# Overlapping window extraction: the index arithmetic ahead of the loads, one copy moved between engines, and the last store as plain transfers

## The chip, the cores and the metric

The kernel runs on one core of one Trainium2 chip. The metric is device time in microseconds (us). The core has the vector engine (DVE), the scalar engine (ACT), GpSimd (POOL) and the sync engine (SP), which work side by side, and sixteen DMA engines that move data between the chip's main memory and the on-chip buffer of 128 partitions. DMAs are issued here by two of them: POOL, whose descriptors are made in software (queue `software_dynamic`), and SP (queue `hardware_dynamic`).

## The reference

The input is an image batch `x[16, 64, 64, 64]` (batch, channel, height, width; float32). Windows of 8 x 8 are cut from it at a stride of 4, so 15 x 15 windows an image, and each is copied out whole, with all channels:

```
for i in range(n_h):
    for j in range(n_w):
        h_start = i * stride
        w_start = j * stride
        result[:, i, j] = x[:, :, h_start:h_start + window_size, w_start:w_start + window_size].copy()
```

No arithmetic is done. 16.8 MB are read and 16 x 225 windows of 16 KB, 59 MB, are written.

## The kernel before

**The image on the chip.** `L` holds all of `x`. A partition holds one channel half `ch` (32 channels), one image `b` and one quarter of the height `q` (16 rows): partition = `ch * 64 + b * 4 + q`. The loads are sorted by batch half `y` (8 images each) and by quarter `q`: for each of the eight pairs, SP loads channels 4 to 31 of the first channel half, and POOL the other four of them and all of the second half. One load thus fills eight partitions, four apart (line 57).

**The tiles that go out.** Four buffers `G[0..3]` of 128 partitions each hold one complete window a partition (64 channels x 8 x 8, 16 KB). Partition `half * 64 + b * 4 + q` holds the window of row `4 * q + s + half` and column `j`, where `s` is 0 or 2. So a pair `(j, s)` is one tile, and 2 x 15 pairs make the output. With `s = 2` the row would be 15 for `half = 1, q = 3`, which does not exist; those 16 partitions have an index that lies out of bounds, so nothing is written for them.

**`fill` (lines 127 to 139)** makes one half of a tile by two copies out of `L`, one for each channel half; its argument `copies` names who makes them (`act` is ACT, `dve` is DVE). For the fourth row of a quarter (`s + half = 3`) the window reaches into the next partition, so a copy of the upper four image rows and a `stream_shuffle` on DVE of the lower four stand in place of one copy.

**`scatter` (lines 114 to 125)** stores a tile by one indirect DMA on POOL's queue, with an index tile that gives each partition its row of the output. The index tiles (`idx` and four variants: `idx_y0`, `idx_y1` for one batch half alone, `idx_hi`, `idx_lo` for the pairs with `s = 2`) come from an `iota` on POOL and some twenty tiny operations on DVE (lines 70 to 107).

**The order.** In the program the loads come first, then iota and index arithmetic, then eight memsets of tile parts that the first stores do not fill, then the tiles. The first three tiles are stored for each batch half separately (six stores of 64 windows: the first three need only the first half's loads, the next three the second's), then 27 whole pairs follow: `j` from 0 to 14, in each `s = 0` (from `j = 3` on) and `s = 2`. Tile number `t` uses buffer `G[t % 4]`, so a fill waits until the store four tiles before has landed. Each engine executes its own instructions in an order that the framework fixes when the kernel is built, which need not be the program's; the framework also sets the waits between engines.

Of the kernel before, what the change touches and what calls it, by code (L numbers as in the profile page):

```python
# [1 line left out]

# [4 lines left out]


@with_exitstack  # L10
def kernel(
    ctx: ExitStack,
    tc: tile.TileContext,
    x: bass.AP,
    window_size: int,
    stride: int,
    out: bass.AP,
):
    nc = tc.nc
    P = nc.NUM_PARTITIONS  # L20

    B, C, H, W = x.shape
    Bo, NH, NW, Co, WSo, WSo2 = out.shape
    WS = int(window_size)
    ST = int(stride)
    assert Bo == B and Co == C and WSo == WS and WSo2 == WS

    f32 = mybir.dt.float32
    i32 = mybir.dt.int32
    ALU = mybir.AluOpType  # L30
    CH = 2
    HQ = P // (B * CH)
    CL = C // CH
    RB = H // HQ
    NSLOT = RB // ST
    NWIN = NH * NW
    CFREE = C * WS * WS
    HP = P // CH
    YB = 8
    NY = B // YB  # L40
    QP = YB * HQ
    assert HQ == 4 and WS == 2 * ST and QP == 32 and NSLOT == 4

    lpool = ctx.enter_context(tc.tile_pool(name="lpool", bufs=1))
    ipool = ctx.enter_context(tc.tile_pool(name="ipool", bufs=1))
    gpool = ctx.enter_context(tc.tile_pool(name="gpool", bufs=1))


    L = lpool.tile([P, CL, RB, W], f32)
    x_v = x.rearrange("(y b) (ch cl) (hq r) w -> ch y hq b cl (r w)", y=NY, ch=CH, hq=HQ)  # L50


    SMALL = 4

    def load(eng, ch, y, q, c0, c1):
        p0 = ch * HP + y * QP + q
        eng.dma_start(out=L[p0 : p0 + QP - HQ + 1 : HQ, c0:c1, :, :], in_=x_v[ch, y, q, :, c0:c1, :])  # L57

    for y in range(NY):
        for q in range(HQ):  # L60
            load(nc.sync, 0, y, q, SMALL, CL)
            load(nc.gpsimd, 0, y, q, 0, SMALL)
            load(nc.gpsimd, 1, y, q, 0, CL)

    def itile(name):
        return ipool.tile([P, 1], i32, name=name)

    pi, tb, tq, tc_, th, idx, idx_y0, idx_y1, idx_lo, idx_hi = (  # L70
        itile(n) for n in ("pi", "tb", "tq", "tc", "th", "idx", "idx_y0", "idx_y1", "idx_lo", "idx_hi")
    )
    FAR = float(2 * B * NWIN)
    nc.gpsimd.iota(pi[:, :], pattern=[[0, 1]], base=0, channel_multiplier=1)  # L74

    def bits(d, shift, mask):
        nc.vector.tensor_scalar(out=d[:, :], in0=pi[:, :], scalar1=shift, scalar2=mask, op0=ALU.logical_shift_right, op1=ALU.bitwise_and)  # L77

    def mul(d, a, m):
        nc.vector.tensor_scalar(out=d[:, :], in0=a[:, :], scalar1=float(m), scalar2=None, op0=ALU.mult)  # L80

    def tt(d, a, b, op):
        nc.vector.tensor_tensor(out=d[:, :], in0=a[:, :], in1=b[:, :], op=op)  # L83

    bits(tb, 2, B - 1)
    bits(tq, 0, HQ - 1)
    bits(tc_, 6, 1)
    mul(tb, tb, NWIN)
    mul(th, tq, NSLOT * NW)
    tt(tb, tb, th, ALU.add)  # L90
    mul(th, tc_, NW)
    tt(idx, tb, th, ALU.add)

    bits(th, 5, 1)
    mul(th, th, FAR)
    tt(idx_y0, idx, th, ALU.add)
    nc.vector.tensor_scalar(out=th[:, :], in0=th[:, :], scalar1=-1.0, scalar2=FAR, op0=ALU.mult, op1=ALU.add)
    tt(idx_y1, idx, th, ALU.add)

    nc.vector.tensor_scalar(out=tq[:, :], in0=tq[:, :], scalar1=float(HQ - 1), scalar2=FAR, op0=ALU.is_equal, op1=ALU.mult)  # L100
    tt(th, tc_, tq, ALU.mult)
    tt(idx_hi, idx, th, ALU.add)
    nc.vector.tensor_scalar(out=tc_[:, :], in0=tc_[:, :], scalar1=-1.0, scalar2=1.0, op0=ALU.mult, op1=ALU.add)  # L103
    tt(th, tc_, tq, ALU.mult)
    tt(idx_lo, tb, th, ALU.add)
    mul(th, tc_, NW)
    tt(idx_lo, idx_lo, th, ALU.add)

    o_v = out.rearrange("b i j c r w -> (b i j) (c r w)")
    nxt = [min(p + 1, 31) for p in range(32)]  # L110
    NG = 4
    G = [gpool.tile([P, C, WS, WS], f32, name=f"G{n}") for n in range(NG)]

    def scatter(g, ix, j, s):
        st = nc.gpsimd.indirect_dma_start(  # L115
            out=o_v,
            out_offset=bass.IndirectOffsetOnAxis(ap=ix[:, 0:1], axis=0),
            in_=g.rearrange("p c r w -> p (c r w)"),
            in_offset=None,
            element_offset=(s * NW + j) * CFREE,  # L120
            bounds_check=B * NWIN - 1,
            oob_is_err=False,
        )
        tc.declare_no_dep(st.ins, group="stores", reason="each store writes rows of its own")
        tc.add_to_no_dep_group("stores", st.ins)

    def fill(g, half, s, j, lo, n, copies):

        d = slice(half * HP + lo, half * HP + lo + n)
        cols = slice(j * ST, j * ST + WS)  # L130
        for ch in (half, 1 - half):
            f = slice(ch * HP + lo, ch * HP + lo + n)
            cs = slice(ch * CL, (ch + 1) * CL)
            copy = copies[ch != half]
            if s < NSLOT - 1:
                copy(out=g[d, cs, :, :], in_=L[f, :, s * ST : s * ST + WS, cols])  # L136
            else:
                copy(out=g[d, cs, 0:ST, :], in_=L[f, :, s * ST : RB, cols])  # L138
                nc.vector.stream_shuffle(out=g[d, cs, ST:WS, :], in_=L[f, :, 0:ST, cols], mask=nxt)  # L139

    act, dve = nc.scalar.copy, nc.vector.tensor_copy

    EARLY = 3
    assert EARLY < NG
    for t in range(NG):
        for half in range(CH):
            p0 = half * HP + (QP if t < EARLY else 0)
            nc.vector.memset(G[t][p0 : p0 + QP, :, :, :], 0.0)  # L150
    t = 0
    for y in range(NY):
        for j in range(EARLY):
            for half in range(CH):
                fill(G[t % NG], half, half, j, y * QP, QP, (act, dve))
            scatter(G[t % NG], (idx_y0, idx_y1)[y], j, 0)
            t += 1

    units = [(j, s) for j in range(NW) for s in (0, 2) if s or j >= EARLY]
    for j, s in units:  # L160
        g = G[t % NG]
        t += 1
        if s == 0:
            for half in range(CH):
                fill(g, half, s + half, j, 0, HP, (act, dve))
            scatter(g, idx, j, s)
        else:

            turn = j % 2
            fill(g, turn, s, j, 0, HP, (act, act))  # L170
            fill(g, 1 - turn, s + 1, j, 0, HP, (dve, dve))
            scatter(g, (idx_hi, idx_lo)[turn], j, s)


# [1 line left out]
_INS = ['x', 'window_size', 'stride']  # L176
_OUTS = [((16, 15, 15, 64, 8, 8), 'float32')]

_NUMBERS = {'window_size': 8, 'stride': 4}


# [26 lines left out]
```

## Time and profile before

| what | value |
|---|---|
| median of 3 runs | 203.56 us (203.37 to 203.70) |
| the profiled execution | 203.62 us, of which the span of the profile is 201.8 |
| DMA, POOL's queue | 68.43 MB, 82.6% of sixteen engines' span |
| DMA, SP's queue | 7.34 MB, 9.4% |
| DVE busy | 131.2 us (65%) in 155 instructions |
| ACT busy | 125.5 us (62%) in 67 |
| POOL busy | 52.6 us (26%) in 54 |
| stores | 33 indirect DMAs on POOL |

The span runs from the first instruction to the last event of the core; the time of a run is a little longer. In rows of instructions in order of time stand the start, the duration, the engine, the line, the operation, its operands and count, and in brackets how long the engine had been idle and what released it. SP's and POOL's work as issuers of DMAs is short beside the transfers themselves, which run on after the issue. The engines' shares are means over the whole run; which engine sets the time has to be read stretch by stretch.

### The profile page before, as it was taken

What the parts mean: (1) busy time and instruction counts of PE and PEld (TensorE: products, weight loads), DVE (VectorE), ACT (ScalarE), POOL (GpSimd) and SP (SyncE); (2) the same over time, 40 slices, a digit from 0 to 9 for tenths busy, and PEclk for the clock granted to TensorE, in tenths of its full rate; (3) what the DMA queues carried; (4) which work ended last, traced back from release to release, by engine and by line L of the source; (5) the groups of instructions that cost most, each with busy time, mean ns of one, the idle gap of its engine ahead of it and who ended that gap; (6) DMA issues with size and microseconds to landing.
All of it is one profiled execution on the core that took longest, in us unless ns stands there. A gap on an engine that the chain in (4) does not pass through costs nothing.

```text
span 201.8 us, 478 instructions
## 1 busy us (share of the span) xinstructions
DVE 131.2 (65%) x155; ACT 125.5 (62%) x67; POOL 52.6 (26%) x54
## 2 busy tenths in 40 slices
DVE  6778888944559999576757765774757577754000
ACT  0000019924259999999977977797777779774000
POOL 7311220200433312613422211323133214311000
DMA  2999999993299899999999999999999999999980
GB/s 93 337 406 399 401 399 400 398 397 98 104 409 406 330 390 412 409 422 416 414 416 429 430 416 416 419 416 432 425 419 416 416 422 432 425 419 414 416 373 36
DMA packets 11476, 75.81 MB, mean 376 GB/s; under 512 B 3776, under 2 KB 3776, under 8 KB 7872
## 3 DMA queue, kind: packets, MB, share of 16 engines
q0 software_dynamic: 9616, 68.43, 82.6%
q1 hardware_dynamic: 1856, 7.34, 9.4%
q14 instruction: 4, 0.03, 0.0%
HBM read 16.78 MB, written 69.21 MB: 426 GB/s over the span
## 4 chain that ended last, share of the span: by engine, by line
DMA 65%; issue 8%; DVE 7%; ACT 7%; POOL 3%; POOLq 1%; DVEq 0%; PEldq 0%; ACTq 0%
DMA out_dram<-G,idx 20%; DMA L<-in_x_dram 16%; DMA out_dram<-G,idx_hi 14%; DMA out_dram<-G,idx_lo 12%; ACT G L136 7%; DVE G L136 4%; DMA out_dram<-G,idx_y 3%; POOL L L57 2%; DVE G L139 2%; POOL out_dram L115 1%; DVE G L138 1%; POOLq L203 1%; DVE th L80 0%; DVE idx_y L83 0%; POOLq L115 0%
## 5 line engine op out<-in xcount | busy, mean ns | idle before, releaser
L136 ACT COPY G<-L 64x2048 f32<-64x2048 f32 (+1 forms) x66 | 124.2, 1896 | 28.9 <-DMA out_dram<-G,idx 10.1
L136 DVE COPY G<-L 64x2048 f32<-64x2048 f32 (+1 forms) x36 | 43.9, 1227 | 22.8 <-DMA out_dram<-G,idx 12.7
L139 DVE STREAM_SHUFFLE G<-L 64x1024 f32<-64x1024 f32 x30 | 38.3, 1276 | 0.0
L138 DVE COPY G<-L 64x1024 f32<-64x1024 f32 x30 | 20.7, 691 | 21.4 <-DMA out_dram<-G,idx_hi 14.4
L150 DVE MEMSET G<- 32x4096 f32 x8 | 27.8, 3472 | 8.0 <-issue 5.4
L115 POOL DMA_INDIRECT out_dram<-G,idx x12 | 13.8, 1149 | 34.7 <-ACT G L136 29.2
L115 POOL DMA_INDIRECT out_dram<-G,idx_hi x8 | 11.7, 1459 | 31.1 <-DVE G L139 17.9
L136 ACT ACT_TABLE_LOAD x1 | 1.3, 1283 | 29.4 <-DMA L<-in_x_dram 29.4
L57 POOL DMA_DIRECT2D L<-in_x_dram x16 | 9.9, 625 | 25.2 <-DMA L<-in_x_dram 24.3
L115 POOL DMA_INDIRECT out_dram<-G,idx_lo x7 | 8.9, 1278 | 18.8 <-ACT G L136 9.7
L115 POOL DMA_INDIRECT out_dram<-G,idx_y x6 | 6.9, 1152 | 22.9 <-DVE tc L103 16.1
L74 POOL IOTA pi<- 128x1 int32 x1 | 1.2, 1230 | 0.1
L83 DVE TENSOR_TENSOR th<-tc,tq 128x1 int32<-128x1 int32 x2 | 0.3, 174 | 0.1
L83 DVE CUSTOM_DVE_ANT_0 idx_y<-idx,th 128x2 uint16<-128x2 uint16 x2 | 0.3, 158 | 0.1
L80 DVE TENSOR_SCALAR th<-tc 128x1 int32<-128x1 int32 x2 | 0.3, 153 | 0.0
L139 DVE LOAD_MASK_SELECT G<-L x30 | 0.2, 6 | 0.0
L83 DVE CUSTOM_DVE_ANT_0 idx_hi<-idx,th 128x2 uint16<-128x2 uint16 x1 | 0.2, 159 | 0.0
L83 DVE CUSTOM_DVE_ANT_0 idx<-tb,th 128x2 uint16<-128x2 uint16 x1 | 0.2, 159 | 0.0
L83 DVE CUSTOM_DVE_ANT_0 idx_lo<-tb,th 128x2 uint16<-128x2 uint16 x1 | 0.2, 159 | 0.0
L83 DVE CUSTOM_DVE_ANT_0 idx_lo<-idx_lo,th 128x2 uint16<-128x2 uint16 x1 | 0.2, 159 | 0.0
L83 DVE CUSTOM_DVE_ANT_0 tb<-tb,th 128x2 uint16<-128x2 uint16 x1 | 0.2, 158 | 0.0
L77 DVE TENSOR_SCALAR th<-pi 128x1 int32<-128x1 int32 x1 | 0.2, 154 | 0.0
(13 smaller groups left out, 1.8 us busy)
## 6 DMA issues: line engine op xcount, KB each, us to landing
L<-in_x_dram POOLq DMA_DIRECT2D x8, 1024.0 KB, 21.2
L<-in_x_dram SPq DMA_DIRECT2D x8, 896.0 KB
L<-in_x_dram POOLq DMA_DIRECT2D x8, 128.0 KB, 21.1
out_dram<-G,idx POOLq DMA_INDIRECT x12, 14.6
out_dram<-G,idx_hi POOLq DMA_INDIRECT x8, 14.0
out_dram<-G,idx_lo POOLq DMA_INDIRECT x7, 14.1
out_dram<-G,idx_y POOLq DMA_INDIRECT x6, 6.3
```

What stands on the lines that cost most here:

```text
L57: eng.dma_start(out=L[p0 : p0 + QP - HQ + 1 : HQ, c0:c1, :, :], in_=x_v[ch, y, q, :, c0:c1, :])
L74: nc.gpsimd.iota(pi[:, :], pattern=[[0, 1]], base=0, channel_multiplier=1)
L77: nc.vector.tensor_scalar(out=d[:, :], in0=pi[:, :], scalar1=shift, scalar2=mask, op0=ALU.logical_shift_right, op1=ALU.bitwise_and)
L80: nc.vector.tensor_scalar(out=d[:, :], in0=a[:, :], scalar1=float(m), scalar2=None, op0=ALU.mult)
L83: nc.vector.tensor_tensor(out=d[:, :], in0=a[:, :], in1=b[:, :], op=op)
L115: st = nc.gpsimd.indirect_dma_start(out=o_v, out_offset=bass.IndirectOffsetOnAxis(ap=ix[:, 0:1], axis=0), in_=g.rearrange("p c r w -> p (c ...
L136: copy(out=g[d, cs, :, :], in_=L[f, :, s * ST : s * ST + WS, cols])
L138: copy(out=g[d, cs, 0:ST, :], in_=L[f, :, s * ST : RB, cols])
L139: nc.vector.stream_shuffle(out=g[d, cs, ST:WS, :], in_=L[f, :, 0:ST, cols], mask=nxt)
L150: nc.vector.memset(G[t][p0 : p0 + QP, :, :, :], 0.0)
L203: with _tile.TileContext(nc) as tc:
```

## The change

Three things change.

1. The block that issues the loads is moved in the program behind the iota and the index arithmetic.
2. In the second batch half, for the second tile (`j == 1`) and its second half, both copies are DVE's; before, one was ACT's and one DVE's.
3. The last two pairs change places, so `(14, 2)` is stored before `(14, 0)`, and this last tile, 128 windows or 2.1 MB, is not stored by the indirect DMA on POOL but by eight plain transfers on SP's queue, one for each quarter and half. Each takes the sixteen partitions of one half that are four apart, one for each image.

```diff
-    for y in range(NY):
-        for q in range(HQ):
-            load(nc.sync, 0, y, q, SMALL, CL)
-            load(nc.gpsimd, 0, y, q, 0, SMALL)
-            load(nc.gpsimd, 1, y, q, 0, CL)
...
     tt(idx_lo, idx_lo, th, ALU.add)

+    for y in range(NY):
+        for q in range(HQ):
+            load(nc.sync, 0, y, q, SMALL, CL)
+            load(nc.gpsimd, 0, y, q, 0, SMALL)
+            load(nc.gpsimd, 1, y, q, 0, CL)
...
+    def free(st):
+        tc.declare_no_dep(st.ins, group="stores", reason="each store writes rows of its own")
+        tc.add_to_no_dep_group("stores", st.ins)
...
             for half in range(CH):
-                fill(G[t % NG], half, half, j, y * QP, QP, (act, dve))
+                copies = (dve, dve) if y and half and j == 1 else (act, dve)
+                fill(G[t % NG], half, half, j, y * QP, QP, copies)
...
     units = [(j, s) for j in range(NW) for s in (0, 2) if s or j >= EARLY]
+    units.append(units.pop(-2))
+    o_q = out.rearrange("b i j c r w -> i j b (c r w)")
...
-            scatter(g, idx, j, s)
+            if (j, s) != units[-1]:
+                scatter(g, idx, j, s)
+                continue
+            g_q = g.rearrange("(ch b q) c r w -> ch q b (c r w)", ch=CH, q=HQ)
+            for q in range(HQ):
+                for half in range(CH):
+                    free(nc.sync.dma_start(out=o_q[q * NSLOT + s + half, j], in_=g_q[half, q]))
```

`free` holds the two lines that `scatter` had: it tells the framework that the stores do not depend on each other.

3 lines of the change are left out of this document (1 added, 2 removed).

## The prediction

> **What bounds the kernel now.** I read four views in this order: the page's forty slices (is one resource full, and where does it fall away), the stretches around the hole that they show, the chain that ended last (who makes the hole), and the instructions in order of time (what each engine did meanwhile).
>
> ```profile
> DMA  2999999993299899999999999999999999999980
> GB/s 93 337 406 399 401 399 400 398 397 98 104 409 406 330 390 412 409 422 416 414 416 429 430 416 416 419 416 432 425 419 416 416 422 432 425 419 414 416 373 36
> ```
>
> The DMA engines are the bound: nine tenths or more in nearly every slice, except the first, slices ten and eleven (98 and 104 GB/s), the small sag at slice fourteen (330) and the last. So time can be won only where the DMA engines stand idle. Columns of the next view: stretch, its length, busy time of DVE, ACT and POOL with counts, granted clock, DMA share, GB/s.
>
> ```profile
> 3.00:4.00 1.00, 1.00 (x1) 0.00 (x0) 1.00 (x2) 1.00 0.49 188
> 4.00:5.00 1.00, 1.00 (x1) 0.00 (x0) 1.00 (x3) 1.00 0.51 197
> ...
> 47.00:48.00 1.00, 0.00 (x0) 0.01 (x1) 0.00 (x0) 1.00 0.08 9
> ...
> 47.30:54.20 6.90, 5.17 (x23) 3.79 (x2) 1.07 (x1) 1.00 0.00 0
> 54.20:54.80 0.60, 0.00 (x0) 0.00 (x0) 0.47 (x1) 1.00 1.03 437
> ...
> 62.40:70.30 7.90, 7.67 (x13) 7.80 (x5) 3.10 (x3) 1.00 0.90 370
> 70.30:71.70 1.40, 1.37 (x4) 1.38 (x2) 0.19 (x1) 1.00 0.66 281
> ...
> 90.00:195.00 105.00, 62.64 (x80) 77.54 (x42) 26.81 (x21) 1.00 1.01 422
> ...
> 195.90:198.10 2.20, 0.00 (x0) 0.00 (x0) 0.00 (x0) 1.00 0.44 186
> ...
> 198.90:201.80 2.90, 0.00 (x0) 0.00 (x0) 0.00 (x0) 1.00 0.00 0
> ```
>
> Loads end at about 47.1 us; then not a byte moves until about 54.6, a hole of 7.5 us. A second, partial loss follows from 62.4 to 71.7: 7.9 x 0.10 + 1.4 x 0.34 = 1.3 us. From 90 to 195 the DMA engines are full at 422 GB/s, while DVE and ACT are busy 63 and 78 of 105 us, so a store of 128 windows (2.10 MB) takes 4.97 us and one of 64 takes 2.49. In that stretch nothing else can set the time: whatever is gained before 72 us is carried to the end unchanged. At the end one half of the engines runs 2.2 us longer than the other (share 0.44), and 2.9 us follow the last byte.
>
> ```profile
> 42.60 5.25 issue
> ...
> 49.29 1.22 DVE G L136
> ...
> 50.54 0.15 DVE tb L77
> ...
> 52.85 0.07 DVE tc L103
> ...
> 52.95 0.40 POOL out_dram L115
> ```
>
> This is the chain, with start and length of each piece: it shows who makes the hole: DVE's last copies of the fourth tile, then the index arithmetic (lines 77 to 103), and only then the first store, since its index tile did not exist. The same stretch in order of time, by engine:
>
> ```profile
> 1.65 3.47 DVE L150 MEMSET G<- 32x4096 f32 x1 [1.65 <-PEq L189]
> 6.04 3.47 DVE L150 MEMSET G<- 32x4096 f32 x1 [0.91 <-issue]
> ...
> 30.69 11.01 ACT L136 COPY G<-L 32x2048 f32<-32x2048 f32 x6
> 34.88 0.66 POOL L57 DMA_DIRECT2D L<-in_x_dram  x1 [4.88 <-DMA L<-in_x_dram]
> 35.63 1.23 POOL L74 IOTA pi<- 128x1 int32 x1
> 35.67 6.93 DVE L136 COPY G<-L 32x2048 f32<-32x2048 f32 x6
> 47.98 3.82 ACT L136 COPY G<-L 32x2048 f32<-32x2048 f32 x2 [6.28 <-issue]
> 48.04 2.47 DVE L136 COPY G<-L 32x2048 f32<-32x2048 f32 x2 [5.44 <-issue]
> ...
> 52.95 1.07 POOL L115 DMA_INDIRECT out_dram<-G,idx_y  x1 [16.09 <-DVE tc L103]
> ...
> 53.56 0.16 DVE L83 CUSTOM_DVE_ANT_0 idx_lo<-idx_lo,th 128x2 uint16<-128x2 uint16 x1
> 57.67 5.12 DVE L136 COPY G<-L 32x2048 f32<-32x2048 f32 x4 [3.96 <-DMA out_dram<-G,idx_y]
> 57.73 17.28 ACT L136 COPY G<-L 32x2048 f32<-32x2048 f32 x9 [5.92 <-DMA out_dram<-G,idx_y]
> ...
> 69.51 0.98 POOL L115 DMA_INDIRECT out_dram<-G,idx_hi  x1 [2.88 <-ACT G L136]
> ```
>
> The three tiles of the first batch half were filled by 42.6, ten microseconds before their first store could go. From 52.95 (issue) to 54.6 (data) a store needs 1.65 us. The first store's landing at 57.67 then releases the tile for the fifth fill.
>
> **Index tiles first.** POOL: the iota, 1.23 us, now stands ahead of the sixteen POOL loads. SP's loads do not wait for it: between 3 and 5 us they alone keep half of the DMA engines busy (0.49, 0.51). So between none and all of 1.23 us is lost to the loads that only POOL carries, the second channel half; I take all of it for copies that read that half, none for the others. DVE: the arithmetic, 50.54 to 53.72 = 3.2 us, moves from behind the eighth copy to the front of the memsets (the first may still precede it, as the iota ends near 2.6). The eight memsets, 4.38 us apart, and the six copies behind them move by 3.2: copies end at 45.8 in place of 42.6. Cover: no store can flow before the loads leave the POOL queue at 47.1. Filled tile by tile, the tiles are ready at 41.2, 43.5 and 45.8, and the third is not needed until 47.1 + 2 x 2.6 - 1.65 = 50.6; if the copies go by halves, the first is ready at 43.5 against 45.4 needed. With that cover gone it would cost up to 3.2. POOL also has to have issued its last load (34.88, now up to 36.1), which is earlier than any of these.
>
> The stores of the first half then run right behind the loads, 47.1 (or up to 48.3) onward, 2.6 each by the spacing of their first landings (57.67, 60.30 below); they land at about 51.4, 54.0 and 56.6 counting the whole 1.23.
>
> ```profile
> 54.33 5.97 DMA out_dram<-G,idx_y
> 60.30 0.02 issue
> ```
>
> The groups of instructions by line and shape give the prices of the copies (after the bar: busy us, then mean ns of one):
>
> ```profile
> L139 DVE STREAM_SHUFFLE G<-L 64x1024 f32<-64x1024 f32 x30 | 38.3, 1276 | 0.0
> ...
> L136 ACT COPY G<-L 32x2048 f32<-32x2048 f32 x12 | 22.4, 1895 | 12.3 <-issue 6.3 <-DMA out_dram<-G,idx_y 5.9
> L138 DVE COPY G<-L 64x1024 f32<-64x1024 f32 x30 | 20.7, 691 | 21.4 <-DMA out_dram<-G,idx_hi 14.4 <-DMA out_dram<-G,idx_lo 6.3
> L136 DVE COPY G<-L 32x2048 f32<-32x2048 f32 x12 | 14.3, 1215 | 9.6 <-issue 5.4 <-DMA out_dram<-G,idx_y 4.0
> ```
>
> What is late next are the fills of the second half. I follow them to the seventh tile (the first of two-row stores, issued at 69.51 now), since from there the queue stays full. **Even copies**: the fifth tile gives one of ACT's two copies to DVE. ACT: three copies of 1.90 from 48.0, to 53.7; the sixth tile's buffer comes free at 54.0, two copies, 57.8; the seventh, two, 61.6. DVE, from 48.04 + 1.23 = 49.3: two, three and two copies of 1.215, to 57.8; the seventh, two of 0.69 + 1.28, to 61.7. Both end together; the store goes at 62.0 (before, ACT's sixth copy from 57.73, at 17.28 / 9 = 1.92 each, ended at 69.25 and POOL started 0.26 later), against 69.51: **7.5 us earlier**. Without the moved copy ACT would take 1.9 longer and end the stage alone at 63.5: the even copies are worth 1.5 to 1.9 of the 7.5.
>
> From the side of the DMA engines: loads to 47.1 (one half of the engines up to 48.3), six stores of 2.5 to 2.6, so 62.5 to 63.9, and the seventh store's data at 62.0 + 1.65 = 63.7. A gap of 0 to 1.2 stands where the 7.5 and 1.3 stood, less the iota's 0 to 1.2: a gain between 6.5 and 8.6, with 7.5 inside. I take 7.5, bounds 6.5 and 8.6.
>
> **The last two units change places; eight plain transfers on SP.** The bytes are the same, no new copy is made, and the fills keep their kinds. SP has nothing queued: the waits of its queue show it idle for 168.4 us at the end of the kernel.
>
> ```profile
> SPq L203 <- DMA out_dram<-G,idx: 168.4, 1, 168.4
> ```
>
> The last store before, from the instructions in order of time:
>
> ```profile
> 184.63 0.97 POOL L115 DMA_INDIRECT out_dram<-G,idx_hi  x1 [4.56 <-ACT G L136]
> ```
>
> The last store is issued at 184.63 now and its last byte leaves 13 us later, so a quicker issue (0.97 us on POOL saved) wins nothing. No row shows 16 KB rows leaving on SP. Dear side: SP's 4 KB pieces moved 188 to 197 GB/s on half of the engines, POOL's stores 211 (half of 422); 2.1 MB at twice 197 take 5.3 in place of 4.97, +0.35. Gainful side: if the eight transfers evened out the two halves' ends, half of 2.2 us: -1.1. Sixteen rows on sixteen engines give each the same share, as the store of 128 did, so I take neither evening nor loss but the half of the dear end: +0.2. A stall that no such row prices is the first rival.
>
> **Sum.** The profiled execution took 203.62 us (span 201.8, 1.8 around it), 0.06 over the median of 203.56, so nothing is corrected: 203.62 - 7.5 + 0.2 = **196.3**.
>
> **Rivals.** (a) *The SP transfers run at half speed.* Each takes sixteen partitions of one half. The rows at 3 to 5 us show eight partitions of one half at 188 to 197 GB/s; they cannot tell whether eight engines or that half's way out of the buffer is the limit. If the latter, 2.1 MB need 10.6 us instead of 4.97. They leave beside POOL's rows, which use the other half's way as well, so between nothing and all of 5.6 is lost: 196.1 to 201.7, in the middle **198.9**. The point is open, since before no two engines had to draw from the same few partitions. Against: halves alternate from one transfer to the next, so some of it can overlap. The Trainium skill states just this ("SBUF — State Buffer", section "Door 1: The DMA port swizzle"): transfers from 64 partitions of one half reach only 8 of 16 ports and half of the rate; by that rule this rival holds, and no run here shows it yet. Chance 0.30.
> (b) *The early stores hold up the loads.* If their rows took turns with the second half's loads in place of queueing behind them, those loads would end up to 7.8 us later (three stores of 2.6), the fills would start at 55 and the seventh store go near 69: about 203. Against it: the loads of the second channel half and the stores are issued by POOL, one behind the other, and only SP's share of the loads could be overtaken. Chance 0.05.
> (c) *The change does not do what it says: the arithmetic stays late on DVE.* In this trace it ran behind eight copies, though the iota was done at 36.9, so an order that was not readiness put it there. Then only the even copies help: ACT's chain shortens by 1.9, and at most the 1.3 of the second loss returns: 202.4. Chance 0.04.
> (d) *Slower: the SP transfers sit on few engines.* A row takes 4.97 / 8 = 0.62 us. On k engines 128 rows take 128/k x 0.62 in place of eight rows. The first 7.3 us of that only eat the gain, so it decides below k = 6.5: on four engines, 32 rows, 14.9 us more, 211. Against: SP's loads of eight partitions filled half of sixteen engines, so partitions do spread. Chance 0.02.
> (e) *Both halves end together*, with the gain at its bound: 195 or less. Chance 0.04.
>
> **Numbers.** The forecast holds with 0.55. Its own range is 195.3 to 197.3. Downward I stop at 195.3 (leaves out e, 0.04); upward the range takes in most of (a), to 200.8, leaving out its worst part (0.05) and (b), (c), (d): 0.20 in all. About 0.4 us (0.2%) is what a measurement of this kernel can tell from no change. Faster: 0.55 + 0.30 + 0.04 + (c) 0.04, and half of (b) 0.02 = 0.95; same: the rest of (b), 0.03; slower: (d), 0.02.
>
> **What would show it.** Index arithmetic on DVE before 10 us, the iota before POOL's first load; the first store issued near 41 to 44; no stretch with DMA share near zero between 45 and 60; the seventh store issued at 62.0, ACT and DVE ending its fill within 0.5 of each other; DMA near 420 GB/s from 72 on. If rival (a) is right, the last 15 us show full DMA share with clearly fewer GB/s. The forecast falls if the fills start later than 49.3, if the DMA hole merely moves to the second half's first store, or if the time from the last SP issue to the end grows.

## The result, and the profile after

The changed kernel runs at 196.82 us (median of 4; before 203.63 beside it), ratio 0.9667 (0.965 to 0.9684), so 6.8 us faster; the forecast was 196.3. The profiled execution took 196.84, its span is 195.1. The page's slices first:

```profile
DMA  2999999999999999999999999999999999999983
GB/s 87 316 403 403 398 402 394 403 399 408 420 375 380 386 420 403 427 420 415 430 430 415 417 417 420 423 423 420 430 423 420 420 427 410 410 418 420 329 259 124
```

The hole of slices ten and eleven is gone. But something new stands at the end: 329 and 259 GB/s at a DMA share that the line above still gives as nine and eight tenths. Instructions of the changed kernel in order of time (start, duration, engine, line):

```profile
0.84 0.12 POOL L68 IOTA pi<- 128x1 int32 x1 [0.39 <-PEq L216]
1.48 5.02 POOL L57 DMA_DIRECT2D L<-in_x_dram  x8 [0.52 <-issue]
...
9.54 0.15 DVE L71 TENSOR_SCALAR tb<-pi 128x1 int32<-128x1 int32 x1
...
38.55 0.16 DVE L77 CUSTOM_DVE_ANT_0 idx_lo<-idx_lo,th 128x2 uint16<-128x2 uint16 x1
38.93 7.00 DVE L139 COPY G<-L 32x2048 f32<-32x2048 f32 x6 [0.22 <-issue]
44.53 1.53 POOL L119 DMA_INDIRECT out_dram<-G,idx_y  x1 [8.54 <-DVE G L139]
...
48.08 28.56 ACT L139 COPY G<-L 32x2048 f32<-32x2048 f32 x15 [5.94 <-issue]
48.13 8.62 DVE L139 COPY G<-L 32x2048 f32<-32x2048 f32 x7 [2.20 <-issue]
...
61.67 0.96 POOL L119 DMA_INDIRECT out_dram<-G,idx_hi  x1 [2.88 <-ACT G L139]
...
171.50 0.96 POOL L119 DMA_INDIRECT out_dram<-G,idx_hi  x1 [3.79 <-ACT G L139]
173.06 3.82 ACT L139 COPY G<-L 64x2048 f32<-64x2048 f32 x2 [2.35 <-DMA out_dram<-G,idx_hi]
...
174.98 14.82 SPq L179 DMA_DIRECT2D out_dram<-G  x8
```

The first store goes at 44.53 (52.95 before), the fills of the second half start at 48.1 as soon as their loads are in, and the seventh store goes at 61.67 (69.51 before): 7.84 us earlier. The stretches of the changed kernel (length, DVE, ACT, POOL, clock, DMA share, GB/s; a row counts whole in the stretch in which it begins, so a share can pass 1):

```profile
47.00:48.00 1.00, 0.00 (x0) 0.00 (x0) 0.69 (x2) 1.00 1.12 447
48.00:54.00 6.00, 5.77 (x5) 5.87 (x4) 3.30 (x2) 1.00 1.03 434
54.00:55.00 1.00, 0.97 (x2) 1.00 (x1) 0.37 (x1) 1.00 0.48 181
...
60.00:65.00 5.00, 4.90 (x8) 4.95 (x3) 0.96 (x1) 1.00 0.89 370
...
72.00:176.00 104.00, 71.21 (x92) 86.76 (x47) 28.69 (x23) 1.00 1.01 421
176.00:179.50 3.50, 0.00 (x0) 0.87 (x1) 0.00 (x0) 1.00 1.03 431
179.50:190.00 10.50, 0.00 (x0) 0.00 (x0) 0.00 (x0) 1.00 0.93 295
190.00:194.00 4.00, 0.00 (x0) 0.00 (x0) 0.00 (x0) 1.00 0.53 164
...
193.90:195.10 1.20, 0.00 (x0) 0.00 (x0) 0.00 (x0) 1.00 0.00 0
```

From 72 to 179.5 full share means 421 to 431 GB/s. Then, with SP's rows among POOL's, a share of 0.93 moves only 295: the engines are occupied but each row takes longer. And behind the last byte 1.2 us follow, where 3.1 did before (last byte at 198.7, span 201.8; the row in the prediction begins a little later, hence its 2.9). So the tail shows a loss and a gain that the total hides.

### The profile page after: what moved, and what is told of

Same layout as the page of the kernel before. It is cut to its first block, busy times and chain, and to the rows that moved or that the text cites. A ratio compares the mean times of both kernels' runs of the same rounds, so it can differ in the third digit from the quotient of the medians.

```text
span 195.1 us, 485 instructions
## 1 busy us (share of the span) xinstructions
DVE 132.0 (68%) x156; ACT 123.6 (63%) x66; POOL 51.8 (27%) x53
## 4 chain that ended last, share of the span: by engine, by line
DMA 66%; DVE 17%; issue 3%; POOL 2%; ACTq 1%; ACT 1%; DVEq 0%; PEldq 0%
DMA out_dram<-G,idx 21%; DMA L<-in_x_dram 18%; DMA out_dram<-G,idx_hi 15%; DMA out_dram<-G,idx_lo 12%; DVE G L139 8%; DVE G L142 6%; DVE G L141 2%; POOL L L57 2%; ACTq L216 1%; ACT G L139 1%; DVEq L139 0%; POOL pi L68 0%; DVEq L141 0%; PEldq L216 0%; ACTq L139 0%
## 5 line engine op out<-in xcount | busy, mean ns | idle before, releaser
L139 ACT COPY G<-L 64x2048 f32<-64x2048 f32 (+1 forms) x65 | 122.3, 1896 | 23.5 <-DMA out_dram<-G,idx 9.9
L139 DVE COPY G<-L 64x2048 f32<-64x2048 f32 (+1 forms) x37 | 44.8, 1221 | 16.7 <-DMA out_dram<-G,idx 11.4
L119 POOL DMA_INDIRECT out_dram<-G,idx x11 | 11.4, 1040 | 30.6 <-ACT G L139 30.6
L119 POOL DMA_INDIRECT out_dram<-G,idx_y x6 | 9.4, 1559 | 13.4 <-DVE G L139 8.5
L68 POOL IOTA pi<- 128x1 int32 x1 | 0.1, 125 | 0.4 <-PEq L216 0.4
```

What stands on the lines that cost most here:

```text
L119: st = nc.gpsimd.indirect_dma_start(out=o_v, out_offset=bass.IndirectOffsetOnAxis(ap=ix[:, 0:1], axis=0), in_=g.rearrange("p c r w -> p (c ...
```

## The experiments

All ratios are against the kernel before, timed beside each. Theory throughout: the front gained about 8 us, and the tail took back a little over one, as the sum of a loss at shared ports and a gain in the closing.

| kernel | median us | ratio (95% interval) |
|---|---|---|
| changed kernel | 196.82 | 0.9667 (0.965 to 0.9684) |
| new front, old tail | 195.47 | 0.9601 (0.9588 to 0.9613) |
| new tail alone | 205.08 | 1.0073 (1.0061 to 1.0085) |
| new front without even copies, old tail | 197.82 | 0.9721 (0.9708 to 0.9733) |
| even copies alone | 202.86 | 0.9963 (0.9951 to 0.9976) |
| new front, pairs swapped, no SP | 195.37 | 0.9595 (0.9582 to 0.9608) |
| SP for one half, eight partitions a transfer | 195.85 | 0.9618 (0.9605 to 0.9631) |
| the same, late | **193.72** | 0.9513 (0.950 to 0.9526) |
| new front, halves exchanged in the last pair | 194.40 | 0.955 (0.9536 to 0.9564) |
| late, sixteen partitions | 194.26 | 0.9539 (0.9526 to 0.9552) |

**New front, old tail.**

```diff
-    units.append(units.pop(-2))
...
-            if (j, s) != units[-1]:
-                scatter(g, idx, j, s)
-                continue
-            g_q = g.rearrange("(ch b q) c r w -> ch q b (c r w)", ch=CH, q=HQ)
-            for q in range(HQ):
-                for half in range(CH):
-                    free(nc.sync.dma_start(out=o_q[q * NSLOT + s + half, j], in_=g_q[half, q]))
+            scatter(g, idx, j, s)
```

> The loads stand behind the index arithmetic and the fifth tile's copies are even, as in the changed kernel; the last two pairs are in their old order and both leave by POOL's indirect stores. Theory: the front of the change gained 8.0 us (the store of the thirtieth tile leads by that much in the changed kernel's trace) and the tail took back 1.2, so this runs at 203.6 - 8.0 = 195.6 us, faster than the changed kernel by 1.2, with rows of 0.62 us to the end and some 2.9 us behind the last byte, as before. Rival: the tail cost nothing and the lead was lost by the two halves of the engines drifting apart, as they do before: then 196.8.

195.47: the front is worth 203.67 - 195.47 = 8.2 us, and the tail of the changed kernel costs 1.35. Stretches of this kernel:

```profile
72.00:176.00 104.00, 71.27 (x92) 87.58 (x47) 28.52 (x23) 1.00 1.01 421
176.00:187.50 11.50, 0.10 (x1) 0.00 (x0) 0.96 (x1) 1.00 0.99 415
187.70:190.20 2.50, 0.00 (x0) 0.00 (x0) 0.00 (x0) 1.00 0.38 164
...
190.80:193.90 3.10, 0.00 (x0) 0.00 (x0) 0.00 (x0) 1.00 0.00 0
```

The last byte leaves before 190.8, in the changed kernel at 193.9: the SP transfers cost 3.1 us of transfer. The closing is 3.1 against 1.2: 1.9 come back. Net 1.2 in the spans. What the closing is, the waits of SP's queue show, this kernel's first, then the changed kernel's (waited for: total, times, longest; PEq is the matmul engine's sequencer, whose signal came last there):

```profile
SPq L209 <- DMA out_dram<-G,idx_hi: 4.5, 1, 4.5
SPq L209 <- PEq L209: 2.5, 2, 2.0
```

```profile
SPq L216 <- DMA out_dram<-G,idx_hi: 2.2, 1, 2.2
...
SPq L216 <- DMA out_dram<-G: 1.7, 3, 0.6
...
SPq L216 <- PEq L216: 0.7, 2, 0.5
```

The wait for the other engines at the end is 2.0 us where POOL's store comes last and 0.5 where SP's does. The traces' records name the engine: POOL's closing drain (a DRAIN among its last instructions) ends 2.0 us after POOL's own last store has landed: 201.05 after 199.00 before the change, 193.13 after 191.08 in this kernel, 194.03 after 192.02 in the changed one. If SP's rows are still on their way then, those 2.0 us pass beside them.

**New tail alone.** The kernel before with the swapped pairs and the SP transfers.

```diff
+    units.append(units.pop(-2))
...
+            g_q = g.rearrange("(ch b q) c r w -> ch q b (c r w)", ch=CH, q=HQ)
+            for q in range(HQ):
+                for half in range(CH):
+                    free(nc.sync.dma_start(out=o_q[q * NSLOT + s + half, j], in_=g_q[half, q]))
```

> The kernel before with only its tail changed: last two pairs swapped, the last tile by eight transfers on SP. Theory: sixteen partitions of one half make two engines draw from one port, so the transfers cost 2.9 us, and 1.6 come back because POOL's closing drain (2.0 us after its last store has landed) is no longer last: 203.6 + 1.2 = 204.8, with a stretch of full DMA share at 260 to 330 GB/s before the end. Rival: the tail is neutral, 203.6 within 0.4.

205.08, so 1.4 slower by itself. Its stretches:

```profile
187.00:198.50 11.50, 0.00 (x0) 0.00 (x0) 0.00 (x0) 1.00 0.88 313
...
201.20:203.20 2.00, 0.00 (x0) 0.00 (x0) 0.00 (x0) 1.00 0.00 0
```

The same slow stretch. In the records the last row ends at 201.19, 2.6 later than before the change (198.59), and 1.3 return (closing 2.0 against 3.3). POOL's last store lands at 200.37 here, only 0.8 before the last row ends, where it was 1.8 in the changed kernel; so less of its drain is covered. The net is near what was expected, its two parts are smaller.

**No even copies.** The new front and old tail with `(act, dve)` for every tile.

```diff
-                copies = (dve, dve) if y and half and j == 1 else (act, dve)
-                fill(G[t % NG], half, half, j, y * QP, QP, copies)
+                fill(G[t % NG], half, half, j, y * QP, QP, (act, dve))
```

> As the first kernel here, but without the even copies: ACT makes both of its copies for the fifth tile. Theory: ACT is the bound between the loads and the seventh store, so that store goes 1.5 to 1.9 us later (63.2 to 63.6 in place of 61.7) and the run ends at 197.1 to 197.5. Rival: the stores of the first batch half give the DMA engines enough work to cover it: 195.6, the same as the first.

197.82, above the range given: the even copies are worth 2.35 us, more than the 1.5 to 1.9 expected, and the early index tiles without them 203.67 - 197.82 = 5.85. This kernel, the seventh store and the stretch around it, then the same two of the one with even copies:

```profile
63.71 1.12 POOL L119 DMA_INDIRECT out_dram<-G,idx_hi  x1 [2.78 <-ACT G L139]
```

```profile
60.00:66.00 6.00, 5.91 (x12) 5.93 (x4) 2.06 (x2) 1.00 0.53 220
```

```profile
61.63 0.96 POOL L119 DMA_INDIRECT out_dram<-G,idx_hi  x1 [2.88 <-ACT G L139]
```

```profile
60.00:66.00 6.00, 5.91 (x10) 5.93 (x4) 1.49 (x2) 1.00 0.95 396
```

The store waits for ACT, and it goes 2.08 later. Once the hole is closed, ACT's chain is the bound, and every us of it stands as idle DMA engines: share 0.53 in place of 0.95, which over 6 us is a loss of 2.5.

**Even copies alone.** The edit is the last one's reverse, in the kernel before.

> The kernel before with the even copies alone. Theory: the hole of 7.5 us stays; ACT's chain behind it gets 1.9 shorter, and of the 1.3 us lost between 62.4 and 71.7 nearly all returns: 202.3 to 202.8. Rival: DVE takes ACT's place as the bound there (three copies of 1.22 and two shuffles in a row) and nothing returns: 203.6.

202.86, 0.8 faster, 0.06 above the range given. In order of time:

```profile
57.67 6.26 DVE L136 COPY G<-L 32x2048 f32<-32x2048 f32 x5 [3.96 <-DMA out_dram<-G,idx_y]
...
60.37 7.66 ACT L136 COPY G<-L 32x2048 f32<-32x2048 f32 x4 [0.75 <-DMA out_dram<-G,idx_y]
...
68.57 0.97 POOL L115 DMA_INDIRECT out_dram<-G,idx_hi  x1 [2.90 <-ACT G L136]
```

The seventh store leads by 0.94, not 1.9: ACT is done early with the fifth tile but then waits (0.75) for the sixth buffer's store to land. The two edits at the front help each other: 0.8 alone, 2.35 behind the early index tiles.

**Pairs swapped, no SP.** The changed kernel with `scatter(g, idx, j, s)` for its last tile.

> The changed kernel with its last two pairs still swapped, but the last tile by POOL's indirect store: only the SP transfers are taken out. Theory: the swap by itself moves nothing, since each engine has the same rows: 195.5 within 0.3, as the kernel with the whole old tail (195.47). Rival: the swap carries part of the tail's cost: between 195.8 and 196.8.

195.37: the swap moves nothing. The whole cost of the tail lies in the SP transfers.

**SP for one half, eight partitions a transfer.** SP sends only partitions 0 to 63, eight partitions a transfer; POOL sends the others with an index tile that puts the first 64 out of bounds.

```diff
+            g0 = g
+            fill(g0, 0, s, j, 0, HP, (act, dve))
+            fill(g, 1, s + 1, j, 0, HP, (act, dve))
+            scatter(g, idx_h1, j, s)
             for q in range(HQ):
-                for half in range(CH):
-                    free(nc.sync.dma_start(out=o_q[q * NSLOT + s + half, j], in_=g_q[half, q]))
+                for y in range(NY):
+                    p0 = y * QP + q
+                    free(nc.sync.dma_start(out=o_q[q * NSLOT + s, j, y * YB : (y + 1) * YB], in_=g0[p0 : p0 + QP - HQ + 1 : HQ].rearrange("p c r w -> p (c r w)")))
```

> The changed kernel with another last store: SP sends only the half of the tile on partitions 0 to 63, as eight transfers of eight partitions, which land on eight engines with a port each; POOL's indirect store sends the other half with an index tile that leaves out the first (two more tiny operations on DVE). Theory: what made the SP transfers dear is two engines on one port, so every row takes 0.62 us again and the 1.2 to 1.4 come back; but SP's rows alternate with POOL's older rows, so POOL's last store lands at the very end and its 2.0 us of drain stand there as in the kernels without SP: 195.2 to 195.7. Rival: SP's 16 KB rows are slow in themselves, or its queue is: 196.5 or more.

195.85, 0.15 above the range given and under the rival's. The stretches:

```profile
179.50:187.50 8.00, 0.00 (x0) 0.00 (x0) 0.00 (x0) 1.00 0.97 410
...
190.70:193.90 3.20, 0.00 (x0) 0.00 (x0) 0.00 (x0) 1.00 0.00 0
```

410 GB/s with SP's rows among POOL's, where the changed kernel had 295; 64 rows of the same size on the same queue. So neither SP nor the row size is slow. The closing is 3.2 again, since POOL's last store landed last (191.09 in the records, SP's 190.91) and its drain ended at 193.14.

**The same, late.** SP's half goes into the buffer of the tile two before, `G[(t + 1) % NG]`, which comes free only at 181.4.

```diff
+            g0 = G[(t + 1) % NG]
+            fill(g0, 0, s, j, 0, HP, (act, dve))
```

> As the last one, but SP's half of the tile is filled into the buffer of the tile two before, so that it is ready only after that store has landed (about 180.5 us) and its rows come behind POOL's. Theory: no port is shared, POOL's last store lands some 2.3 us before the last byte, and its drain is covered: the last byte leaves near 190.5, 1.0 us of closing follow, 193.4 to 194.0 for the run, faster than all so far. Rival: the late fill leaves the engines idle before SP's rows, or the drain is not what closed the kernel: 195.5 or more.

193.72, faster than the changed kernel by 3.1 and than the kernel before by 9.9. The stretches, the one half of the engines that SP's rows still occupy and the closing behind them:

```profile
188.00:190.50 2.50, 0.00 (x0) 0.00 (x0) 0.00 (x0) 1.00 0.39 164
...
190.90:192.00 1.10, 0.00 (x0) 0.00 (x0) 0.00 (x0) 1.00 0.00 0
```

The last byte leaves where it does without SP, and the closing is 1.1. In the records POOL's last store lands at 187.98 and its drain ends at 190.03, before SP's last transfer lands at 191.12. This shows the drain by itself: the same bytes, rows of the same length, 2.1 us less than in the experiment before.

**Halves exchanged in the last pair.** New front and old tail, `turn` exchanged for `j == 14`.

```diff
-            turn = j % 2
+            turn = j % 2 if j < NW - 1 else 1 - j % 2
```

> The kernel with the new front and the old tail (195.47), with the two halves exchanged in the last pair, so that the sixteen missing windows fall to the half of the DMA engines that ends last. Theory: that half has two rows less (1.24 us), the other two more; the ends, 188.0 and 190.3 to 191.3 now, meet near 189.2 to 190: 194.2 to 194.6. Rival: the two ends are set by when buffers come free, not by rows: 195.5.

194.40: 1.07 faster than the same kernel without it, a little less than the 1.24 of two rows. The stretch in which one half ran alone is gone:

```profile
179.50:188.30 8.80, 0.00 (x0) 0.00 (x0) 0.00 (x0) 1.00 0.98 417
188.30:189.50 1.20, 0.00 (x0) 0.00 (x0) 0.00 (x0) 1.00 0.04 14
```

**Late, sixteen partitions.** The disputed cost by itself.

```diff
+            g_q = g0.rearrange("(ch b q) c r w -> ch q b (c r w)", ch=CH, q=HQ)
             for q in range(HQ):
-                for y in range(NY):
-                    p0 = y * QP + q
-                    free(nc.sync.dma_start(out=o_q[q * NSLOT + s, j, y * YB : (y + 1) * YB], in_=g0[p0 : p0 + QP - HQ + 1 : HQ].rearrange("p c r w -> p (c r w)")))
+                free(nc.sync.dma_start(out=o_q[q * NSLOT + s, j], in_=g_q[0, q]))
```

> The disputed cost by itself: the last kernel but one of the list so far (SP's half of the tile ready late, 193.72), with the same 64 rows of partitions 0 to 63 sent by four transfers of sixteen partitions in place of eight of eight. Each transfer now runs on sixteen engines, so each engine has four rows and not eight. Theory: the 64 partitions have eight ports, each shared by two engines; a row takes 1.2 us in place of 0.61, full DMA share shows half the GB/s, and the last byte leaves at 190.2 to 191, as with eight engines: 193.4 to 194.0. Rival: engines are the limit, not ports: a row stays at 0.61, SP's rows take 2.5 us instead of 4.9, and the run ends 1 us or more earlier, 192.7 or less, held up only by POOL's drain.

194.26, half a us slower than with eight partitions. The same stretch as two experiments above:

```profile
188.00:190.50 2.50, 0.00 (x0) 0.00 (x0) 0.00 (x0) 1.00 0.76 216
```

Twelve engines at work (0.76 of sixteen) move 216 GB/s, where six (0.39) moved 164. Twice the engines on the same 64 partitions brought no earlier end: SP's last row ends at 190.97, against 190.77. In the trace's records the 64 rows take 0.61 to 1.25 us each, half of them 0.75 or more, against 0.61 to 0.62 with eight partitions. So the number of engines is not the limit. Nor is it SP's queue alone, for POOL's own rows slow down beside such transfers: after 178 us, 51 of 145 of them last longer than 0.65 us in the changed kernel (up to 1.33), and 8 of 273 in the kernel with the new front and the old tail (up to 0.72). What is left is the partitions' way out. The records do not say which engine carried which row, so which engines share a way is not shown.

## Why the prediction was right

**The sum held partly by compensation.** 203.6 - 7.5 + 0.2 was forecast; the two parts measured 203.67 - 8.2 and + 1.35. The front gave 0.7 more and the tail cost 1.15 more than forecast; that the total is off by only 0.5 is luck in this respect.

**Index tiles first: right, the iota mis-sized.** The hole went. The iota was charged with 1.23 us, its duration before; at the head of the queue it takes 0.12 and POOL's first load starts at 1.48 in place of 1.38. So DVE's fills start at 48.13, not 49.3. The seventh store was forecast for 62.0 and goes at 61.67. The step from there to the end was slightly short too: "From 90 to 195 the DMA engines are full" left out the stretch from 72 to 90, where the kernel before still lost a little (406 GB/s at a share of 0.97 from 71.7 to 90) and the changed kernel runs at 1.01. That is the 0.36 between 7.84 and 8.2, argued and not tested by itself.

**The arithmetic on DVE** did not stand in a block before 10 us, as forecast, but in pieces between and behind the memsets from 9.54 to 38.71. The 3.2 us behind which the copies moved came out so (38.93 against 35.67), and the copies went by halves: the first store went at 44.53, behind the 41 to 44 given as a sign but inside the 45.4 that was allowed. The cover held. Two figures of the working are off and move nothing: six stores of 2.5 to 2.6 from 47.1 end at 62.1 to 62.7, not from 62.5 on, and the last byte left 14 us after the last issue (198.6 after 184.63), not 13.

**Even copies:** 1.5 to 1.9 forecast, 2.35 measured. ACT ended its part of the seventh tile at 61.39, as worked out (61.6), but DVE already at 60.61, not 61.7, since it had started 1.2 earlier than forecast; they ended 0.8 apart, not within 0.5. The worth was set too low in two places: without the even copies the seventh store came 2.08 later, not 1.5 to 1.9, and another 0.27 was lost behind it, of which the cause stays open.

**The SP tail: the term that was mis-sized.** Forecast +0.2, measured +1.35. Rival (a) holds as a mechanism: the SP rows cost 3.1 us, inside its bounds of 0 to 5.6, near its middle of 2.8. Its sign came too: from 179.5 to 190 a share of 0.93 with only 295 GB/s. The step that failed is "Sixteen rows on sixteen engines give each the same share": each has the same rows, but sixteen engines get little more out of 64 partitions than eight do. That it did not cost 3.1 on the whole is the second thing missed: the forecast saw the 2.9 us that follow the last byte and did not ask what they are. They hold POOL's drain, and SP's late rows cover it. The Trainium skill ("SBUF — State Buffer", section "Door 1: The DMA port swizzle") gives 8 of 16 ports to 64 partitions of one half; the trace of the last experiment agrees roughly, with 216 GB/s on twelve engines beside 211 for half of a full store's 422 (by its records SP's last 48 rows, from 187.67 to 190.97, moved 238 GB/s). The Trainium skill's page "DMA: Bandwidth & Descriptors" (section "Issuing engines are not separate DMA queues") says that issuing from several engines saves only issue time; here it also saved the 2.0 us of POOL's closing, and the measurement decides.

Rivals (b), (c), (d) and (e) did not come: the second half's fills, which wait for the loads, started within 0.1 us of before, the arithmetic was done before the first store, up to sixteen of SP's rows were on their way at once, and the two halves did not end together (share 0.53 in the last 4 us).

## What to carry to other kernels

Before a store is moved to another queue, write down which partitions each DMA engine will draw from: equal rows an engine are not enough if, as here, sixteen engines draw on one half's 64 partitions. Ask also what lies between the last byte and the end of the span; where POOL's DMAs come last, a last small transfer on SP that lands 2 us after them covers POOL's closing. The late transfer and the exchanged halves were not tried together. When a hole in a bound resource is closed, follow the next producer at once: the even copies were worth three times as much behind the closed hole as alone.

## What the runs showed that was not expected

When sixteen DMA engines read from 64 partitions of one half, many 16 KB rows take about 1.2 us in place of 0.61. The DMA share stays high (0.93 in the changed kernel), so only the GB/s beside it tell it (295). POOL's closing drain lasts 2.01 to 2.06 us after its last store lands, in each of the eleven traces. An iota that takes 1.23 us behind sixteen loads takes 0.12 at the head of POOL's queue; why was not tried.
